# Two of eight gate pairs as plain products, a later spread of the roots, and tiles moved by 64 bytes

## The chip, the cores and the metric

The kernel runs on one core of one Trainium2 chip. The metric is the device time of one execution in microseconds (us); the time of a version is the median of its runs. TensorE (PE) does the matmuls, VectorE (DVE), ScalarE (ACT) and GpSimd (POOL) the rest, SyncE (SP) issues most DMAs. Each engine works through its own list of instructions in order, and waits on semaphores for the others.

## The reference

A trunk of two residual layers over 512 tokens of width 1024: a gMLP mixer, an MLP, a forgetting-attention mixer (FoX), an MLP, all float32. What is changed lies in the gMLP mixer (and, by its addresses, behind it):

```python
h = rms_norm(x, mix_norm_g[0])
z = gelu(h @ w_in)                    # (512, 4096)
u, v = split(z, 2, axis=-1)           # 2048 columns each
v = layer_norm(v, ln_g, ln_b)         # over the 2048 columns
s = einsum('gts,bnsgc->bntgc', tril(w_s), v) + b_s   # 128x128 over tokens, 8 groups
x = x + (u * s) @ w_out
```

Then `x = x + square(relu(rms_norm(x) @ w1)) @ w2`, the attention layer, and once more the MLP.

## The kernel before, in words

**Splitting.** Each float32 operand of a matmul is split into a high part (a copy by ACT, `wh`, `xh`, `th`, `zh`) and a low part (the difference, by DVE or POOL, `wl`, `xl`, `tl`, `zl`); a product is three matmuls, high by high, high by low, low by high (`mm3`, L275 for each matmul).

**The stream of weights.** `Stream` holds one list of weight chunks of 128 x 1024 (512 KB) for the whole kernel. `take()` hands out the next, keeps three more split ahead, and three loads ahead of those. Raw chunks have three places (`raw`), split ones four (`wh`, `wl`). L96 is a load, L99 the ACT half of a split, L100 the DVE half.

**Products by sevens.** Most products of the widening layers are made in pairs of 128 output rows by a scheme with seven products of half size (two blocks of rows, two halves of the depth, two halves of the 512 tokens) in place of eight. It needs sums of weight blocks and sums of token blocks. In the gMLP the weight sums are made on POOL in the places of the two raw chunks (`_sums_in_place`, L126 to L129), when the second chunk has been split ("end": only half of it is split for itself), and then count as two more chunks, "S31" and "S24". The token sums are `th`, `tl` (`gth`, `gtl` in the profile).

**The gMLP stage** goes in this order on TensorE: `pv`, the first half of the v columns in plain products, in two blocks `g` of four chunks `c`; within it the norm's sums of squares (`nps`, L317 to L329 with the root on POOL) and, four small multiplications, the spread of the roots over the partitions (`spread`, `npb`); `va` to `vd`, the second half of v by sevens; then what `GMLP_ORDER` lists. In that list `("uu", n, a, b, c, d)` is pair n of 128-column blocks of u by sevens (`gate_pair`, products `da` and `bc`, joined by DVE on L570 and L574, then scaled by the roots on L416 and put through gelu on L417), a to d being blocks whose mixing is issued behind the first two, the third and fourth, the fifth and sixth, and the seventh product. `("w", q)` loads mixing weights, `("s", n)` issues mixing n, and `("o", g, m)` is a chunk of the output product with blocks 4g to 4g+3 (`po`).

**A mixing** (`mix`) scales a block of v by the layer norm (`lnr`, `lnm`, ACT L623), splits it (`vh` ACT L626, `vl` POOL L627), multiplies by the mixing weights (`sp`, L640 and L641), applies gain and bias (`b` L630, `zt` L643 and L644 on DVE), multiplies by u (POOL L646) and splits the result (`zg` ACT L653, `zl` DVE L654). The load of `bs` on L618 serves two mixings.

**Order.** The program text is not the order on the engines: a planner sorts instructions by what its model of the engines holds ready, within the dependencies. The FoX stage is pinned.

**Places.** Tiles lie in pools, one behind another in each partition: `const`, `wp` (chunks), `xp` (x, `xh`, `xl`), `small`, and on top of these in turn `gp` with `vp` or `gq` (gMLP), `mp` (MLP) and `fs` with `fp` (FoX). A tile takes a multiple of 32 bytes in each partition, so the length of `small` sets the addresses in all pools behind it. In the program before, `small` ends at byte 123584, 192 past a multiple of 256; behind `lngb` (128 bytes), or a filling tile `pad`, the tiles follow at 64 past one.

```python
def take(self):
    i = self.taken
    self.prefetch(i + 1 + self.ahead)
    self.taken += 1
    return self.parts.pop(i)
```

Of the kernel before, what the change touches and what calls it, by code (L numbers as in the profile page):

```python
# [8 lines left out]
F32 = mybir.dt.float32  # L9
F32R = mybir.dt.float32r  # L10
AF = mybir.ActivationFunctionType
# [5 lines left out]
P = 128  # L17
# [3 lines left out]
NT = S // P  # L21
# [21 lines left out]
WARM = 8  # L43


GMLP_ORDER = [("w", 0), ("uu", 0, None, None, None, None), ("uu", 1, None, None, 0, None), ("uu", 2, None, 1, 2, None)]
GMLP_ORDER += [("uu", 3, 3, None, None, None), ("o", 0, 0), ("s", 4), ("o", 0, 1), ("s", 5), ("o", 0, 2), ("o", 0, 3)]
GMLP_ORDER += [("uu", 4, 6, 7, None, None), ("w", 1), ("o", 1, 0), ("o", 1, 1)]
GMLP_ORDER += [("uu", 5, 8, 9, None, None), ("o", 1, 2), ("o", 1, 3)]
# [118 lines left out]
def trunk(ctx: ExitStack, tc: tile.TileContext, A, out, stages=4):  # L168
# [10 lines left out]
    def psA(name):  # L179
        return ps.tile([P, S], F32, tag="A", name=name, bufs=4)  # L180
# [12 lines left out]
    chunks = []  # L193
# [5 lines left out]
    for q in (1, 2, 4, 3):  # L199
        chunks += [((q, c), None) for c in range(2)]  # L200
    for kind, *at in GMLP_ORDER:
        if kind == "uu":
            chunks += [(A["gw_u"][2 * at[0]], "begin"), (A["gw_u"][2 * at[0] + 1], "end"), ("S31", None), ("S24", None)]
        elif kind == "o":
            chunks += [A["gw_o"][at[0], at[1]]]
# [150 lines left out]
    def dense_a(dst, w, nm, pin=False):  # L356

        wh, wl = (t.rearrange("p (k m) -> p k m", m=P) for t in w)
        for k in range(KB):
            mm3(dst, wh[:, k], wl[:, k], nm.h[k], nm.l[k], k == 0, k == KB - 1, pin and k == 0)  # L360
# [26 lines left out]
    nm = Norm(0)  # L387
# [8 lines left out]
    with ExitStack() as st:  # L396
# [1 line left out]

        lngb = gp.tile([P, 2, E // P], F32, tag="lngb", name="lngb")
        nc.sync.dma_start(lngb, A["ln_gb"])  # L400
        onesr = gp.tile([P, P], F32R, tag="onesr", name="onesr")
        act.activation(onesr, ones, AF.Copy)

        v = [gp.tile([P, 4, NT, P], F32, tag=f"v{g}", name=f"v{g}") for g in range(4)]
        th, tl = ([gp.tile([P, 4, HS], F32R, tag=f"t{w}{k}", name=f"gt{w}{k}") for k in range(4)] for w in "hl")
        bn = small.tile([P, NT, 4, 6], F32, tag="bn", name="bn")
        tok = [slice(i * P, (i + 1) * P) for i in range(NT)]
        us = {}

        def u_place(b, dt, name):  # L410

            return gq.tile([P, S], dt, tag=f"u{b % 8}", name=f"{name}{b}")

        def gated(pu, u):

            dve.tensor_tensor(u, pu, nm.rbc, op=ALU.mult)  # L416
            act.activation(u, u, AF.Gelu_apprx_tanh)  # L417

        with ExitStack() as st2:
# [44 lines left out]
            for g in range(2):  # L464
                pv = [(psB if g == 1 and i < 3 else psA)(f"pv{g}_{i}") for i in range(NT)]
                for c in range(4):
                    wh, wl = (t.rearrange("p (k n) -> p k n", k=2) for t in ws.take())
                    for i in range(NT):
                        for kk in range(2):
                            k = 2 * c + kk  # L470
                            mm3(pv[i], nm.h[k][:, tok[i]], nm.l[k][:, tok[i]], wh[:, kk], wl[:, kk], k == 0, k == KB - 1)
                    if g == 0 and c == 2:
                        with tc.issue_after(fourth):
                            for b in range(KB):
                                nm.square(b)
                        nm.finish()
                    if g == 0 and c == 3:
                        nm.spread()
                        with tc.issue_after(nm.squared.ins):
                            for k in range(4):  # L480
                                token_sums(k)
                    if g == 0 and c > 1:
                        with tc.issue_after(ws.issued[2 * c + 2].ins):
                            load_parts(c - 2)
                    if g == 1 and c in (1, 2):
                        sum_parts(c - 1)
                for i in range(NT):
                    normal(i, g, blocks(pv[i]))
# [51 lines left out]
        dve.tensor_scalar(lnv, mv[:, :, 1], LN_EPS, None, op0=ALU.add)  # L540
        lnr = small.tile([P, NT], F32, tag="lnr", name="lnr")
        pool.tensor_tensor(lnr, lnv, mhalf[:, :NT], op=ALU.pow)
        lnm = small.tile([P, NT], F32, tag="lnm", name="lnm")
        lnm_made = dve.scalar_tensor_tensor(lnm, mv[:, :, 0], -1.0, lnr, op0=ALU.mult, op1=ALU.mult)

        def gate_pair(n):
# [52 lines left out]
        def mixing_weights(q):  # L599

            wT = small.tile([P, 4, P], F32, tag="sq", name=f"wsT{q}", bufs=2)
            nc.sync.dma_start(wT, A["w_sT"][4 * q : 4 * q + 4].rearrange("g s t -> s g t"))
            pool.affine_select(wT, wT, pattern=[[0, 4], [1, P]], compare_op=ALU.is_ge, fill=0.0, base=0, channel_multiplier=-1)
            wsb = gq.tile([P, 4, 2, P], F32R, tag="wsb", name=f"wsb{q}")
            pool.tensor_scalar(wsb[:, :, 0], wT, 1.0, None, op0=ALU.mult)
            pool.tensor_tensor(wsb[:, :, 1], wT, wsb[:, :, 0].bitcast(F32), op=ALU.subtract)
            now["w"] = wsb

        def mix(cb):
            g = cb // 2 % 4  # L610
            wsb = now["w"]
            if cb % 8 == 0:
                now["rs"] = psD(f"rs{cb}")
                for w in range(2):
                    pe.matmul(now["rs"].rearrange("p (g t) -> p g t", g=4), onesr, wsb[:, :, w], start=w == 0, stop=w == 1)
            if cb % 2 == 0:
                now["b"] = gq.tile([P, P], F32, tag="bs", name=f"bs{cb}", bufs=2)
                nc.sync.dma_start(now["b"], A["b_s"][cb // 2].partition_broadcast(P))  # L618

            vb = v[cb // 4][:, cb % 4]  # L620
            with tc.issue_after(now["vh"]) if cb else ExitStack():
                for i in range(NT):
                    act.activation(vb[:, i], vb[:, i], AF.Identity, scale=lnr[:, i : i + 1], bias=lnm[:, i : i + 1])  # L623
            vh = gq.tile([P, NT, P], F32R, tag="vh", name=f"vh{cb}", bufs=2)
            vl = gq.tile([P, NT, P], F32R, tag="vl", name=f"vl{cb}")
            now["vh"] = act.activation(vh, vb, AF.Copy).ins  # L626
            pool.tensor_tensor(vl, vb, vh.bitcast(F32), op=ALU.subtract)  # L627
            b2 = gq.tile([P, P], F32, tag="b2", name=f"b2{cb}", bufs=2)
            with tc.issue_after(lnm_made.ins):
                dve.scalar_tensor_tensor(b2, now["rs"][:, g * P : (g + 1) * P], lngb[:, 1, cb : cb + 1], now["b"], op0=ALU.mult, op1=ALU.add)  # L630
            zt = gq.tile([P, NT, P], F32, tag="zt", name=f"zt{cb}")
            wide = wsb[:, g].rearrange("p w t -> p (w t)")
            gcol = lngb[:, 0, cb : cb + 1]
            for c in range(2):

                sp = psA(f"sp{cb}_{c}")
                s4 = sp.rearrange("p (i w t) -> p i w t", i=2, w=2)
                for i in range(2):
                    dst = sp[:, i * 2 * P : (i + 1) * 2 * P]
                    pe.matmul(dst, vh[:, 2 * c + i], wide, start=True, stop=False)  # L640
                    pe.matmul(dst[:, :P], vl[:, 2 * c + i], wsb[:, g, 0], start=False, stop=True)  # L641
                zc = zt[:, 2 * c : 2 * c + 2]
                dve.scalar_tensor_tensor(zc, s4[:, :, 0], gcol, b2.unsqueeze(1).to_broadcast([P, 2, P]), op0=ALU.mult, op1=ALU.add)  # L643
                dve.scalar_tensor_tensor(zc, s4[:, :, 1], gcol, zc, op0=ALU.mult, op1=ALU.add)  # L644
            zf = zt.rearrange("p i t -> p (i t)")
            pool.tensor_tensor(zf, zf, us[cb], op=ALU.mult)  # L646

            if cb == 0:
                zg[0] = gq.tile([P, 4, S], F32R, tag="zg", name="zg0")
            elif cb % 4 == 0:  # L650
                zg[cb // 4] = gp.tile([P, 4, S], F32R, tag=f"v{cb // 4 - 1}", name=f"zg{cb // 4}")
            h, l = zg[cb // 4][:, cb % 4], u_place(cb, F32R, "zl")
            act.activation(h, zf, AF.Copy)  # L653
            dve.tensor_tensor(l, zf, h.bitcast(F32), op=ALU.subtract)  # L654
            z[cb] = (h, l)

        nxt = Norm(1)
        for kind, n, *at in GMLP_ORDER:
            if kind == "w":
                mixing_weights(n)  # L660
            elif kind == "uu":
                for _, cb in zip(gate_pair(n), at):
                    if cb is not None:
                        mix(cb)
            elif kind == "s":
                mix(n)
            else:
                zs = [z[4 * n + k] for k in range(4)]
                out_chunk(at[0], [t[0] for t in zs], [t[1] for t in zs], 4, 256, nxt.block if n == 3 else None)
# [142 lines left out]
    nm = fx  # L812
# [387 lines left out]
```

## Time and profile before

| | us |
|---|---|
| median of 3 runs | 1280.51 (1279.18 to 1280.64) |
| the profiled execution | 1282.32 |
| its span, first to last instruction | 1280.6 |
| TensorE busy | 1259.1 (98%) |
| VectorE busy | 903.5 (71%) |
| ScalarE busy | 686.0 (54%) |
| GpSimd busy | 524.0 (41%) |
| mean granted TensorE clock | 0.995 of full |

A row of the profile names line, engine, operation, output and inputs; a bracket at its end is the idle time of the engine before it and what ended that. The page gives the busy share of 40 equal slices as digits (9 is 90% or more), for the clock of TensorE the granted share. A line that is a helper's (L275, L99, L100) stands for many uses, which the tile names tell apart.

### The profile page before, as it was taken

What the parts mean: (1) busy time and instruction counts of PE and PEld (TensorE: products, weight loads), DVE (VectorE), ACT (ScalarE), POOL (GpSimd) and SP (SyncE); (2) the same over time, 40 slices, a digit from 0 to 9 for tenths busy, and PEclk for the clock granted to TensorE, in tenths of its full rate; (3) what the DMA queues carried; (4) which work ended last, traced back from release to release, by engine and by line L of the source; (5) the groups of instructions that cost most, each with busy time, mean ns of one, the idle gap of its engine ahead of it and who ended that gap; (6) DMA issues with size and microseconds to landing.
All of it is one profiled execution on the core that took longest, in us unless ns stands there. A gap on an engine that the chain in (4) does not pass through costs nothing.

```text
span 1280.6 us, 19160 instructions
## 1 busy us (share of the span) xinstructions
PE 1259.1 (98%) x7379; PEld 1122.6 (88%) x7379; DVE 903.5 (71%) x1196; ACT 686.0 (54%) x1125; POOL 524.0 (41%) x418
## 2 busy tenths in 40 slices
PE   9998899999999999999999999999999999999998
PEld 8788788988899989898899999898888999999987
DVE  7967877788876767666625666667897767676763
ACT  6666654645544443433457777778465444444430
POOL 3125546536333232310547666667273423223200
PEclk9998899999999999999999999999999999999999
DMA  8502332232332323242223223223213323232321
GB/s 284 190 19 83 104 93 70 90 129 78 116 116 83 118 81 127 72 131 83 70 88 120 86 87 97 86 83 115 91 66 116 112 87 115 83 115 83 116 83 66
DMA packets 42732, 129.08 MB, mean 101 GB/s; under 512 B 5320, under 2 KB 7424, under 8 KB 42640
## 3 DMA queue, kind: packets, MB, share of 16 engines
q1 hardware_dynamic: 42352, 127.83, 30.8%
q8 instruction: 58, 0.95, 0.3%
q14 instruction: 34, 0.28, 0.1%
q10 hardware_dynamic: 288, 0.02, 0.0%
HBM read 125.67 MB, written 2.16 MB: 100 GB/s over the span
## 4 chain that ended last, share of the span: by engine, by line
PE 82%; DVE 7%; POOL 3%; issue 3%; ACT 2%; DMA 1%; SPq 0%; DVEq 0%; POOLq 0%; ACTq 0%
PE po L275 35%; PE da L275 13%; PE bc L275 10%; PE pq L275 9%; PE pg L275 3%; PE ph L275 3%; DVE wl L100 2%; PE pv L275 2%; PE ot L275 2%; PE lg L275 1%; PE va L275 1%; PE tp L280 1%; PE vc L275 1%; ACT wh L99 1%; POOL zt L646 1%
## 5 line engine op out<-in xcount | busy, mean ns | idle before, releaser
L99 ACT ACTIVATE wh<-raw 128x1024 fp32r<-128x1024 f32 (+3 forms) x244 | 229.8, 947 | 199.0 <-PE po L275 82.1
L100 DVE TENSOR_TENSOR wl<-raw,wh 128x1024 fp32r<-128x1024 f32 (+1 forms) x192 | 274.1, 1442 | 24.1 <-ACT wh L99 23.5
L275 PE MATMUL po<-zl,wh 128*128 128x512 f32 x640 | 251.8, 394 | 1.4 <-DVE zl L710 1.4
L275 PE MATMUL po<-zh,wl 128*128 128x512 f32 x512 | 201.9, 394 | 0.0
L275 PE MATMUL po<-zh,wh 128*128 128x512 f32 x512 | 199.6, 391 | 0.0
L766 DVE TENSOR_TENSOR x<-x,po 128x512 f32<-128x512 f32 x128 | 87.3, 683 | 105.9 <-PE po L275 105.9
L100 POOL TENSOR_TENSOR wl<-raw,wh 128x768 fp32r<-128x768 f32 (+3 forms) x52 | 103.2, 1986 | 125.0 <-ACT wh L99 122.5
L139 POOL TENSOR_TENSOR ssum<-raw 128x512 f32<-128x512 f32 x26 | 34.9, 1344 | 273.1 <-DMA raw<-in_m_dram 251.7
L99 ACT ACTIVATE sh<-ssum 128x1024 fp32r<-128x1024 f32 x52 | 55.2, 1061 | 163.1 <-issue 93.2
L275 PEld LDWEIGHTS po<-zl,wh 128*128 128x128 f32 x640 | 120.8, 189 | 24.0 <-DVE zl L710 1.6
L275 PEld LDWEIGHTS po<-zh,wl 128*128 128x128 f32 x512 | 96.4, 188 | 19.0
L275 PEld LDWEIGHTS po<-zh,wh 128*128 128x128 f32 x512 | 96.4, 188 | 18.2
L275 PE MATMUL pq<-wh,xh 128*128 128x384 f32 (+2 forms) x256 | 88.2, 344 | 0.0
L275 PE MATMUL pq<-wh,xl 128*128 128x384 f32 (+2 forms) x256 | 83.1, 325 | 0.0
L275 PE MATMUL pq<-wl,xh 128*128 128x384 f32 (+2 forms) x256 | 82.9, 324 | 0.0
L100 DVE TENSOR_TENSOR sl<-ssum,sh 128x1024 fp32r<-128x1024 f32 x52 | 66.0, 1268 | 18.1 <-ACT sh L99 18.0
L141 POOL TENSOR_TENSOR ssum<-raw,ssum 128x512 f32<-128x512 f32 x26 | 37.2, 1429 | 65.1 <-DVE sl L100 64.8
L275 PE MATMUL da<-th,sl 128*128 128x256 f32 x208 | 59.0, 283 | 0.0
L275 PE MATMUL da<-th,sh 128*128 128x256 f32 x208 | 58.8, 282 | 0.0
L275 PE MATMUL da<-tl,sh 128*128 128x256 f32 x208 | 58.7, 282 | 0.0
L746 DVE TENSOR_TENSOR zc<-da,sl 128x512 f32<-128x512 f32 x26 | 18.0, 692 | 55.1 <-PE da L275 55.1
L142 POOL TENSOR_TENSOR ssum<-raw,raw 128x512 f32<-128x512 f32 x26 | 56.3, 2164 | 0.0
(288 smaller groups left out, 3660.3 us busy)
## 6 DMA issues: line engine op xcount, KB each, us to landing
raw<-in_m_dram SPq DMA_DIRECT2D x128, 512.0 KB, 3.8
raw<-in_gw_u_dram SPq DMA_DIRECT2D x16, 512.0 KB, 3.5
raw<-in_gw_o_dram SPq DMA_DIRECT2D x16, 512.0 KB, 3.6
raw<-in_fw_qkv_dram SPq DMA_DIRECT2D x20, 384.0 KB, 3.1
raw<-in_gw_v_dram SPq DMA_DIRECT2D x12, 512.0 KB, 5.7
gs<-in_gw_v_dram SPq DMA_DIRECT2D x8, 512.0 KB, 7.9
raw<-in_fw_g_dram SPq DMA_DIRECT2D x8, 512.0 KB, 3.6
cb<-cd SPq DMA_DIRECT2D x16, 256.0 KB, 3.4
```

The costliest lines, as they stand in the source:

```text
L99: self.nc.scalar.activation(hi, t, AF.Copy)
L100: eng.tensor_tensor(lo, t, hi.bitcast(F32), op=ALU.subtract)
L139: tt(s12[:, 0], a21, a22, op=ALU.add)
L141: tt(s43[:, 0], a12, s12[:, 1], op=ALU.subtract)
L142: tt(s43[:, 1], a11, a21, op=ALU.subtract)
L275: ins = pe.matmul(dst, a, b, start=start, stop=stop, skip_group_check=more)
L280: placed(pe.transpose(dst, src, ident[: src.shape[0], : src.shape[0]]), 256)
L646: pool.tensor_tensor(zf, zf, us[cb], op=ALU.mult)
L746: dve.tensor_tensor(z[:, 1].rearrange("p (j t) -> p j t", j=2), a.unsqueeze(1).to_broadcast([P, 2, HS]), late.rearrange("p (j t) -> p j t" ...
L766: dve.tensor_tensor(x[b], x[b], pt, op=ALU.add)
```

## The change

- Pairs 0 and 2 of the gate blocks become plain: `("u", n, a, b)` takes one chunk for each block of 128 columns, makes the product with all 512 tokens into one bank (`pu`, `dense_a`, 24 matmuls of 512 columns), and scales and gelus it from there. Their chunks are listed for plain splitting, without sums.
- Mixing 0 is issued behind the fourth part of pair 1, 1 and 2 behind the two products of pair 2. Before, 0 stood behind the third part of pair 1, 1 and 2 behind the second and third of pair 2.
- `spread` is issued in block g = 1 behind chunk c = 1, before in block g = 0 behind chunk c = 3.
- `onesr` is placed behind `v`, `th` and `tl`, and `lnm` is written into the tile of `lnv`, so that `small` is 64 bytes shorter.

```diff
-GMLP_ORDER = [("w", 0), ("uu", 0, None, None, None, None), ("uu", 1, None, None, 0, None), ("uu", 2, None, 1, 2, None)]
+GMLP_ORDER = [("w", 0), ("u", 0, None, None), ("uu", 1, None, None, None, 0), ("u", 2, 1, 2)]
...
     for kind, *at in GMLP_ORDER:
-        if kind == "uu":
+        if kind == "u":
+            chunks += [A["gw_u"][2 * at[0] + e] for e in range(2)]
+        elif kind == "uu":
...
-        onesr = gp.tile([P, P], F32R, tag="onesr", name="onesr")
-        act.activation(onesr, ones, AF.Copy)
-
         v = [gp.tile([P, 4, NT, P], F32, tag=f"v{g}", name=f"v{g}") for g in range(4)]
         th, tl = ([gp.tile([P, 4, HS], F32R, tag=f"t{w}{k}", name=f"gt{w}{k}") for k in range(4)] for w in "hl")
+        onesr = gp.tile([P, P], F32R, tag="onesr", name="onesr")
+        act.activation(onesr, ones, AF.Copy)
...
+                    if g == 1 and c == 1:
+                        nm.spread()
                     if g == 0 and c == 3:
-                        nm.spread()
...
-        lnm = small.tile([P, NT], F32, tag="lnm", name="lnm")
+        lnm = lnv
...
+            elif kind == "u":
+                for b, cb in enumerate(at, 2 * n):
+                    pu = psA(f"pu{b}")
+                    dense_a(pu, ws.take(), nm)
+                    us[b] = u_place(b, F32, "u")
+                    gated(pu, us[b])
+                    if cb is not None:
+                        mix(cb)
```

More of the change, by code (lines that the diff above doesn't have):

```diff
@@ L400, in trunk @@
         nc.sync.dma_start(lngb, A["ln_gb"])
+        v = [gp.tile([P, 4, NT, P], F32, tag=f"v{g}", name=f"v{g}") for g in range(4)]
+        th, tl = ([gp.tile([P, 4, HS], F32R, tag=f"t{w}{k}", name=f"gt{w}{k}") for k in range(4)] for w in "hl")
         onesr = gp.tile([P, P], F32R, tag="onesr", name="onesr")
         act.activation(onesr, ones, AF.Copy)
-        v = [gp.tile([P, 4, NT, P], F32, tag=f"v{g}", name=f"v{g}") for g in range(4)]
-        th, tl = ([gp.tile([P, 4, HS], F32R, tag=f"t{w}{k}", name=f"gt{w}{k}") for k in range(4)] for w in "hl")
         bn = small.tile([P, NT, 4, 6], F32, tag="bn", name="bn")
```

## The prediction

> **What bounds the kernel now.** I read the page first, then the waits of TensorE, then a table of stretches around the place that they point to, then the chain of waits and the timelines there. The page says that TensorE is busy nearly all the time:
>
> ```profile
> span 1280.6 us, 19160 instructions
> PE 1259.1 (98%) x7379; PEld 1122.6 (88%) x7379; DVE 903.5 (71%) x1196; ACT 686.0 (54%) x1125; POOL 524.0 (41%) x418
> PEclk9998899999999999999999999999999999999999
> ```
>
> So there are three ways to a shorter time: fewer or shorter matmuls, less of the 21.5 us in which TensorE is idle (1280.6 less 1259.1), and the two slices (the fourth and fifth, 96 to 160 us) in which the granted clock is under full. The waits of TensorE between 100 and 152 us, in total, times and longest:
>
> ```profile
> PE da L275 <- DVE wl L100: 3.3, 2, 2.8
> PE da L275 <- ACT wh L99: 2.3, 2, 1.9
> PE sp L640 <- DVE zt L644: 2.1, 1, 2.1
> PE bc L275 <- DVE wl L100: 0.5, 1, 0.5
> ```
>
> `wh` and `wl` are the two parts into which a weight chunk is split, `da` and `bc` the products of a gate pair, `sp` a mixing. The stretches (us, then busy us and instructions of PE, PEld, DVE, ACT, POOL, then the granted clock):
>
> ```profile
> 91.60:104.40 12.80, 12.80 (x107) 12.70 (x106) 12.73 (x22) 7.08 (x13) 5.25 (x6) 1.00 0.27 83
> 104.40:112.90 8.50, 5.71 (x40) 4.75 (x39) 5.88 (x11) 8.50 (x18) 5.83 (x4) 1.00 0.21 69
> 112.90:119.80 6.90, 5.51 (x26) 5.51 (x27) 5.11 (x5) 4.74 (x12) 5.06 (x4) 0.51 0.24 76
> 119.80:140.20 20.40, 17.45 (x142) 16.77 (x142) 18.05 (x23) 12.92 (x25) 13.17 (x10) 1.00 0.20 56
> 140.20:143.70 3.50, 3.50 (x19) 3.50 (x19) 1.66 (x3) 3.03 (x8) 3.50 (x2) 0.51 0.27 23
> 143.70:147.10 3.40, 1.54 (x12) 1.34 (x12) 3.06 (x7) 1.96 (x3) 2.63 (x3) 1.00 0.32 133
> 147.10:150.50 3.40, 3.40 (x15) 3.11 (x14) 3.40 (x3) 2.77 (x6) 1.69 (x2) 0.50 0.44 72
> 150.50:260.00 109.50, 108.64 (x681) 97.62 (x681) 84.99 (x124) 59.18 (x106) 55.74 (x39) 1.00 0.32 100
> ```
>
> From 104.4 to 150.5 us TensorE idles 2.79 + 1.39 + 2.95 + 1.86 = 9.0 us, and 5.51 + 3.50 + 3.40 = 12.4 us of its work run at half clock, which loses half of that, 6.2 us. Before and after it hardly waits. These 15.2 us are the gate pairs 0 to 3 and the mixings 0 to 3, and the change rewrites just that.
>
> **The change part by part: pairs 0 and 2 as plain products.** A plain pair is 2 x 8 x 3 = 48 matmuls of 512 columns; a pair by seven products is 7 x 4 x 3 = 84 of 256. Pieces of the chain of waits (start, us, what) price both:
>
> ```profile
> 53.02 5.44 PE va L275 x24
> 69.50 5.60 PE vc L275 x24
> ...
> 149.11 2.14 PE po L275 x6
> ...
> 323.04 5.48 PE ph L275 x24
> ...
> 1234.28 1.44 PE da L275 x12
> 1235.72 1.39 PE bc L275 x12
> ...
> 1241.30 35.74 PE po L275 x156
> ```
>
> `ph` is the plain product of the MLP with the same operands (weights against `xh`, `xl`): 48 matmuls are 10.96 us. 84 at 1.44/12 = 0.120 are 10.08. Two pairs: **+1.8 us** of TensorE work, on the path since TensorE is the bound.
>
> What goes with it is off TensorE: for each of the two pairs four sums on POOL, two splits of 1024 columns on ACT and DVE, two joins on DVE and four copies on ACT, against half a split more, as the second chunk is now split whole. What a split costs DVE alone, what beside POOL, and what that does to TensorE:
>
> ```profile
> 76.72 1.23 DVE L100 TENSOR_TENSOR wl<-gs,wh 128x1024 fp32r<-128x1024 f32 x1 [2.00 <-ACT wh L99]
> 111.99 5.07 DVE L100 TENSOR_TENSOR wl<-raw,wh 128x1024 fp32r<-128x1024 f32 x3
> 114.29 0.58 PE L275 MATMUL da<-gth,wl 128*128 128x256 f32 x1 [2.85 <-DVE wl L100]
> 128.36 0.39 PE L275 MATMUL da<-gth,wl 128*128 128x256 f32 x1 [0.42 <-DVE wl L100]
> 139.69 0.39 PE L640 MATMUL sp<-wsb,vh 128*128 128x256 f32 x1 [2.15 <-DVE zt L644]
> 143.77 1.72 POOL L129 TENSOR_TENSOR raw<-raw 128x512 f32<-128x512 f32 x1
> 146.63 0.38 PE L275 MATMUL da<-gth,wh 128*128 128x256 f32 x1 [1.86 <-ACT wh L99]
> ```
>
> The wait of 2.85 is for pair 1's last chunk of sums, which stood on DVE behind the mixing; the 0.42 is pair 2's; the 1.86 is pair 3's, whose fourth sum ended on POOL only at 145.5. Now pair 0 needs no sums. Pair 1's can be made as soon as its two chunks are there, under 10.96 us of plain product, and a chunk feeds 5.5 us of TensorE, not 1.4 to 2.9: the waits for `wh` and `wl` up to 128.4 go (2.79 + 1.39 + 0.42 = 4.6), and with them the first half-clock stretch (2.75): **-7.35 us**. Bounds: 0, if they come back under the new order, and all of it.
>
> Behind that, pair 3 stays as it is, but pair 2 in front of it asks nothing of POOL. With 11 us of plain product ahead, its sums can be ready some microseconds early (its two chunks land while pair 2 begins, the four sums are 4 x 1.7, the splits need slots that pair 2's own chunks leave at its middle and end). I let the 1.86 and one half-clock stretch (half of 3.50) go: **-3.6 us**. The `sp` wait of 2.15, its companions (0.4) and the other half-clock stretch I leave: it comes from DVE, which had 18.05 us of work in 20.4. The bounds of this part are 0 and 7.8.
>
> The clock: it was halved at 112.9 behind a wait of 2.85, at 140.2 behind 2.15, at 147.1 behind 1.86. The Trainium skill, page "TensorE: Matmul & The Clock Gate", section "HAM oscillation — how this bites in real kernels", has a rule against gaps of over about 3.4 us. The trace differs: no gap here is that long, and the clock fell thrice. By that rule the half-clock stretches would not hang on these waits, and the two terms would be 4.6 and 1.86, a gain 4.5 us smaller.
>
> **The mixings.** Mixing 0 moves from behind the third product of pair 1 to behind the fourth, 1 and 2 behind the two plain products of pair 2. All their instructions (on ACT four scalings and two copies, on DVE six operations, on POOL two, on TensorE eight matmuls and two more for the first, on SP one small load for each two) stay the same in number: 0. They are hidden by the 11 us of pair 2; without that cover each is a wait like the 2.15 above. On SP the small load must not fall behind a chunk load that waits for a slot; there that costs up to
>
> ```profile
> 108.39 16.49 SPq L96 DMA_DIRECT2D raw<-in_gw_u_dram  x3
> ```
>
> three loads over 16.5 us. What waits for it is DVE's `b` in a mixing, and all splits queued behind that.
>
> **The roots spread later.** Now TensorE stands before the third piece of the roots:
>
> ```profile
> 36.87 1.16 PE L275 MATMUL npb<-ident,rstd 128*128 128x128 f32 x8 [0.94 <-POOL rstd L329]
> ```
>
> Moved behind two more chunks of 24 matmuls (10.9 us), the four multiplications find `rstd` ready: **-0.9 us**. Their own 0.9 us and the copy on ACT stay. What could take its place is the next matmul's own wait, for the split of chunk 4 or for a bank; the split is done long before, and three of the four banks of the second block are others than the first's, so I take the full 0.94. Bounds: 0 and 1.1.
>
> **The addresses.** With `lnm` written over `lnv`, the pool `small` loses two 32-byte places. By the address table of the program before, the tiles of `gp`, `gq`, `vp`, `mp` and `fp` start 64 bytes past a multiple of 256, those of `wp` and `xp` on one; now all start on one. `onesr`, 512 bytes, moves the rest by whole multiples: nothing. Does an address cost anything? In the chain above `va` (from `xh`, on the boundary) is 5.44 and `vc` (from `th`, off it) 5.60, with weights alike: 6.7 ns a matmul, for 96 of them 0.6 us. `po`, whose moving operand `zh` or `zl` is off, has 229.1 ns; on it stand `ph` with 228.3 and `va` with 226.7. The counts:
>
> ```profile
> L275 PE MATMUL po<-zl,wh 128*128 128x512 f32 x640 | 251.8, 394 | 1.4 <-DVE zl L710 1.4
> L275 PE MATMUL po<-zh,wl 128*128 128x512 f32 x512 | 201.9, 394 | 0.0
> L275 PE MATMUL po<-zh,wh 128*128 128x512 f32 x512 | 199.6, 391 | 0.0
> ...
> L275 PE MATMUL bc<-xh,sh 128*128 128x256 f32 x104 | 29.1, 280 | 0.0
> ```
>
> 1664 x 0.8 to 2.4 ns is 1.3 to 4.0 us; I take the middle, 2.7, as neither row is the nearer. Against it: the fast 256-column group (1.39 for 12, `xh` with `sh`) has one operand on and one off, the slow one (1.44) both alike; 3 x 104 matmuls that go from the one to the other lose 4.2 ns each, 1.3 us. Together **-2.0 us**; bounds +1.3 and -4.6.
>
> The Trainium skill, page "SBUF — State Buffer", sections "Operand start alignment" and "Who interferes with whom", asks only for element alignment and gives TensorE two read ports that wait for no one. By it this part is 0; the trace's 5.60 beside 5.44 speaks against that.
>
> **The sum.** +1.8 - 7.35 - 3.6 - 0.9 - 2.0 = -12.05 us. The profiled execution took 1282.32 us, span 1280.6 and 1.7 around it: 1270.3. The median of the runs is 1.8 below that execution: **1268.4 us**.
>
> **The rivals.**
> - The later half stays. Pair 3 keeps its sums and DVE its load (18 of 20 us), the 3.6 us don't come: 1272.0. For it: the `sp` wait isn't of the removed work. Against: POOL loses half of its sums there.
> - All goes. The whole 15.2 us are regained and the addresses give the upper bound: 1268.4 less 4.2 less 2.6, 1261.6. For it: beyond 150.5 us, with pairs of the same kind but more matmuls beside them, only 0.9 us in 109.5 are idle.
> - The clock is halved there whatever the waits are, and stays so: the half-clock parts of the two terms (2.75 and 1.75) don't come, 1272.9. Against: the clock is full over the 109.5 us behind, with 0.9 us idle. The Trainium skill's rule above would say this.
> - Addresses don't matter: 1270.4. For it: unlike operands in the rows above; against: 5.60 beside 5.44.
> - Slower: SP stands before a chunk load that waits for a slot, with the small load of mixing 0 behind it; DVE waits in its queue, all splits with it. As long as the 16.49 us above, wholly on TensorE, it gives 1268.4 + 16.5 = 1284.9. It decides from 12.1 + 2.6 = 14.7 us on. Against: chunks now keep their place for one split, not for sums.
> - The waits only move to the first output product, which needs mixings 0 to 3: all of the 11 us come back there, and the time is 1279.4, no change.
>
> **How the numbers follow.** The forecast (waits mostly gone, 1264 to 1271) has 0.50, the later half staying 0.17, all going 0.12, the clock staying low 0.03, the addresses being nothing 0.06, no change 0.05, slower 0.07. 1268.4 is the likeliest. A measurement here tells some 0.2%, 2.6 us, from no change. Faster: 0.50 + 0.17 + 0.12 + 0.03 + 0.06 = 0.88; same 0.05; slower 0.07. The range goes from just under the case in which all goes, 1261, to 1276, where half of the 7.35 also stays: it leaves out the last two cases and little else.
>
> **What would show it.** In the profile after, between 90 and 140 us: no wait of TensorE on `wl` over 1 us and the clock digit of the fourth and fifth slice at 9; the first `po` in the chain some 10 us earlier than 149.1; eight POOL sums of raw up to pair 3 in place of sixteen; no wait for `rstd`; `vc` and `va` from `th` at 5.44 for 24; the `po` run of 156 at the end under 35.74. Wrong I am if TensorE waits for `sp`, `zl` or `wh` by turns in each pair and the clock stays halved, or if the 5.60 stay 5.60.

## The result, and the profile after

| | before | after |
|---|---|---|
| median of 4 runs, us | 1280.05 (1279.18 to 1280.64) | 1271.64 (1271.41 to 1271.99) |
| profiled execution | 1282.32 | 1271.42 |
| its span | 1280.6 | 1269.5 |
| mean granted clock | 0.995 | 0.999 |

The ratio of the times is 0.9935, with an interval of 0.9918 to 0.9952: faster by some 0.65%. A second comparison of the same two kernels, on another chip, gave 1271.02 beside 1280.84, 0.9918 (0.9905 to 0.9932). Each ratio, here and below, is the estimate on record with its interval; it can differ by some 0.1% from the quotient of the two medians. The forecast of 1268.4 was 3.2 us too low; the range held the time.

The page of after, its span, its engines and its clock digits:

```profile
span 1269.5 us, 18988 instructions
PE 1253.6 (99%) x7307; PEld 1117.6 (88%) x7307; DVE 889.3 (70%) x1188; ACT 680.8 (54%) x1113; POOL 509.4 (40%) x410
PEclk9999999999999999999999999999999999999999
```

The two low digits of before are gone, and TensorE is idle for 15.9 us (1269.5 less 1253.6) in place of 21.5. What it waits for between 100 and 152 us (engine, tile and line, what ended the wait, total, times, longest):

```profile
PE po L277 <- DVE x L375: 2.1, 1, 2.1
PE da L277 <- ACT gsl L559: 1.1, 1, 1.1
PE sp L644 <- POOL vl L630: 0.4, 1, 0.4
```

Before, the four groups shown in the prediction summed to 8.2 us, all but 2.1 of it for `wh` and `wl` (two more, of 0.3 each, stood behind them). No wait for a split of weights is left; `vl` is the low half of a block of v in a mixing. The stretches of the same stage (us, busy us and instructions of PE, PEld, DVE, ACT, POOL, granted clock, DMA share, GB/s):

```profile
89.70:109.20 19.50, 18.37 (x108) 16.20 (x106) 14.09 (x26) 13.55 (x27) 9.35 (x7) 1.00 0.18 58
109.20:148.00 38.80, 38.41 (x243) 34.77 (x244) 29.78 (x42) 26.83 (x50) 18.48 (x13) 1.00 0.31 93
148.00:151.30 3.30, 1.15 (x7) 0.85 (x6) 3.30 (x8) 2.56 (x6) 2.67 (x2) 1.00 0.73 245
151.30:154.70 3.40, 3.40 (x10) 2.63 (x9) 1.98 (x3) 0.65 (x2) 0.00 (x0) 0.50 0.05 20
154.70:260.00 105.30, 104.84 (x656) 94.38 (x654) 82.22 (x120) 54.98 (x96) 55.76 (x38) 1.00 0.33 100
```

What is left there is 1.13 us of waiting at 109.2, 0.39 in the second row, 2.15 in the third, and one stretch of 3.40 us at half clock, which loses 1.7: 5.4 us in place of 15.2. DVE's timeline shows what the wait of 2.15 is for:

```profile
143.25 0.68 DVE L577 TENSOR_TENSOR u<-da,gsl 128x512 f32<-128x512 f32 x1
143.85 2.33 DVE L100 TENSOR_TENSOR wl<-raw,wh 128x1024 fp32r<-128x1024 f32 x1
146.11 0.86 DVE L646 SCALAR_TENSOR_TENSOR zt<-sp,lngb,b 128x256 f32<-128x256 f32 x2
146.89 1.21 DVE L100 TENSOR_TENSOR wl<-raw,wh 128x1024 fp32r<-128x1024 f32 x1
148.03 0.68 DVE L418 TENSOR_TENSOR u<-u,rbc 128x512 f32<-128x512 f32 x1
148.63 0.86 DVE L647 SCALAR_TENSOR_TENSOR zt<-sp,lngb,zt 128x256 f32<-128x256 f32 x2
149.41 0.33 DVE L633 SCALAR_TENSOR_TENSOR b<-rs,lngb,bs 128x128 f32<-128x128 f32 x1
149.67 1.86 DVE L375 TENSOR_TENSOR x<-x,po 128x512 f32<-128x512 f32 x3
```

No row has a bracket: DVE works without a gap through pair 3's last join, its scaling, two splits of weights and operations of a mixing, and only then adds the finished output products to `x` and so empties the bank that the next `po` needs.

Where the time went is told by stage. Each column is the distance between two starts of matmuls in the profiled execution, in us: from the first of the norm's sums (`nps`) to the first `va`; v by sevens, from the first `va` to the last; the gate stage, from the last `va` to the first `ph`; the first MLP, from the first `ph` to the first `pg`; and the whole span. The runs of the next section stand in the same table.

| kernel | nps to va | v by sevens | gate stage | first MLP | span |
|---|---|---|---|---|---|
| before | 24.84 | 38.52 | 196.91 | 346.16 | 1280.6 |
| after | 24.84 | 37.85 | 187.39 | 346.13 | 1269.5 |
| after, second profile | 24.33 | 37.85 | 185.68 | 346.13 | 1266.9 |
| before + plain pairs | 24.98 | 38.52 | 187.59 | 346.16 | 1270.7 |
| before + addresses | 24.98 | 37.85 | 196.39 | 346.13 | 1279.0 |
| before + later spread | 24.72 | 38.52 | 197.20 | 346.16 | 1280.0 |
| before + pair 0 plain | 24.60 | 38.52 | 189.93 | 346.16 | 1273.7 |
| after + sums off by 64 | 24.42 | 37.85 | 185.74 | 344.93 | 1265.3 |
| after + sums off by 128 | 24.23 | 37.85 | 186.18 | 346.25 | 1268.0 |
| after + mean first | 23.67 | 37.85 | 185.63 | 346.13 | 1266.6 |
| after + pair 3 plain | 24.78 | 37.85 | 184.02 | 346.13 | 1265.8 |
| after + all three | 23.64 | 37.85 | 183.59 | 344.93 | 1262.0 |

### The profile page after: what moved, and what is told of

Read it like the earlier page. It is cut to its first block, busy times and chain, and to the rows that moved or that the text cites. A ratio compares the mean times of both kernels' runs of the same rounds, so it can differ in the third digit from the quotient of the medians.

```text
span 1269.5 us, 18988 instructions
## 1 busy us (share of the span) xinstructions
PE 1253.6 (99%) x7307; PEld 1117.6 (88%) x7307; DVE 889.3 (70%) x1188; ACT 680.8 (54%) x1113; POOL 509.4 (40%) x410
## 4 chain that ended last, share of the span: by engine, by line
PE 80%; DVE 5%; ACT 2%; POOL 2%; issue 2%; DMA 0%; POOLq 0%; DVEq 0%
PE po L277 35%; PE da L277 13%; PE bc L277 10%; PE pq L277 9%; PE pg L277 3%; PE ph L277 3%; PE ot L277 2%; PE lg L277 2%; DVE xl L305 1%; PE tp L282 1%; DVE wl L100 1%; PE pv L277 1%; ACT wh L99 1%; POOL zt L649 0%; PE sp L643 0%
## 5 line engine op out<-in xcount | busy, mean ns | idle before, releaser
L99 ACT ACTIVATE wh<-raw 128x1024 fp32r<-128x1024 f32 (+3 forms) x240 | 226.6, 949 | 203.8 <-PE po L277 85.5
L100 DVE TENSOR_TENSOR wl<-raw,wh 128x1024 fp32r<-128x1024 f32 (+1 forms) x188 | 265.3, 1424 | 28.9 <-ACT wh L99 28.6
```

The lines of the kernel that those rows point to most:

```text
L99: self.nc.scalar.activation(hi, t, AF.Copy)
L100: eng.tensor_tensor(lo, t, hi.bitcast(F32), op=ALU.subtract)
```

## The experiments

The first four runs take the change apart: each adds one part of it to the kernel before. They ran on one chip, where before had 1281.36.

**The plain pairs alone**, with the mixings' new places (the branch for `"u"` is that of the change):

```diff
-GMLP_ORDER = [("w", 0), ("uu", 0, None, None, None, None), ("uu", 1, None, None, 0, None), ("uu", 2, None, 1, 2, None)]
+GMLP_ORDER = [("w", 0), ("u", 0, None, None), ("uu", 1, None, None, None, 0), ("u", 2, 1, 2)]
```

> The kernel before with only the plain pairs 0 and 2 and their order of mixings. If the gate stage carries nearly all of the gain (theory A): 7.5 to 9.5 us faster than before, the first block of the MLP 9 to 10 us after the last va closer, the v stage (va to its end, 38.5 us) unchanged. If the addresses carry some 2 us of it, as predicted (theory B): only 6 to 7 us faster. If the spread carries 0.9 (theory C): 0.9 less than the whole change.

1271.11 us, 0.9931 (0.9919 to 0.9944): this part alone gives what the change gives. Its gate stage lasts 187.59 us, after's 187.39. Its largest waits of TensorE from 26 to 160 us are after's two, and still the old one for the roots:

```profile
PE po L277 <- DVE x L375: 2.2, 1, 2.2
PE da L277 <- ACT gsl L558: 1.1, 1, 1.1
PE npb L277 <- POOL rstd L331: 1.1, 1, 1.1
```

**Pair 0 alone as plain**, pairs 1 and 2 and all mixings as before (one entry of `GMLP_ORDER`, with the same branch):

```diff
-("uu", 0, None, None, None, None),
+("u", 0, None, None),
```

> The kernel before with pair 0 alone plain, mixings as before. By my walk the waits up to 119.8 us and the first half-clock stretch go (6.9), for 0.9 of more matmuls: -6 us, and the rest of the gain, 2 to 3 us, belongs to pair 2. If the later half depends on pair 2 and the first on both: -2 to -4 us, with a half-clock stretch still there behind pair 1.

1275.16 us, 0.9959 (0.9945 to 0.9972). The gate stage falls by 7.0 us, to 189.93; pair 2, with the mixings' places, gives the other 2.3 (187.59). The four largest waits from 100 to 160 us of this kernel:

```profile
PE da L277 <- ACT wh L99: 2.0, 1, 2.0
PE sp L642 <- DVE zt L646: 1.3, 1, 1.3
PE da L277 <- ACT gsl L558: 1.0, 1, 1.0
PE da L277 <- DVE wl L100: 0.7, 1, 0.7
```

With pair 2 still by sums, a wait for `wh` just before pair 3's last products (2.0 us, of the size of the 1.86 of before) and one for `zt` ahead of it (1.3) stay; with pair 2 plain both are gone. So the second plain pair, together with the mixings' new places, does remove the later waits, as the step said; no run has the one without the other.

**The addresses alone:**

```diff
-        onesr = gp.tile([P, P], F32R, tag="onesr", name="onesr")
-        act.activation(onesr, ones, AF.Copy)
         v = [...]
         th, tl = (...)
+        onesr = gp.tile([P, P], F32R, tag="onesr", name="onesr")
+        act.activation(onesr, ones, AF.Copy)
...
-        lnm = small.tile([P, NT], F32, tag="lnm", name="lnm")
+        lnm = lnv
```

> The kernel before with only the addresses moved by 64 bytes. Theory A: v stage 0.65 us shorter (38.5 to 37.85), each MLP within 0.2 us of before, because po gains about 1.3 ns a matmul and the 256-column products lose about as much in all; total -0.5 to -1.0. Theory B: -2.0 in all, -0.7 or more in each MLP. Addresses mean nothing: 0, and the groups of 24 stay 5.60.

1279.81 us, 0.9993 (0.9985 to 1.0002): no difference that can be told. The stages show why it isn't simply nothing. The chain of this run has the products from `th` at the pace of those from `xh`:

```profile
58.08 5.44 PE vb L275 x24
...
68.96 5.44 PE vc L275 x24
```

`vc` had 5.60, and v by sevens is 0.67 us shorter. But the MLP stays at 346.13 us.

**The later spread alone:**

```diff
+                    if g == 1 and c == 1:
+                        nm.spread()
                     if g == 0 and c == 3:
-                        nm.spread()
```

> The kernel before with only the spread of the roots moved. Theory A: 0 (within 0.3 us), the wait of 0.9 us for rstd replaced by one of about 0.9 for a bank of the second block, which the gelu of the first block frees, and that needs rstd too. Theory C: -0.9 us and no wait between 34 and 42 us.

1281.16 us, 1.0001 (0.9992 to 1.0010): nothing. TensorE's timeline of this kernel has `npb` without a wait, and at the time at which `npb` waited before (36.87) a wait at a product of the next block:

```profile
36.79 0.50 PE L275 MATMUL pv<-wh,xh 128*128 128x512 f32 x1 [0.78 <-ACT v L461]
40.10 1.05 PE L275 MATMUL npb<-ident,rstd 128*128 128x128 f32 x8
```

The second group of runs starts from the kernel after and goes at what the first group left: the MLP that did not move, the wait that took the place of the roots', and the wait for `x`. Three of them and after itself once more ran on another chip (before: 1280.84); the kernel with sums off by 128 bytes and the one with all three parts ran on a third (before: 1281.08).

> The changed kernel again, on the same chip as the three that start from it: 8 to 9 us faster than before.

1271.02 us (1268.73 to 1271.29), 0.9918 (0.9905 to 0.9932). Its profile has the same waits in the gate stage, 2.1 for `x` among them, and yet no half-clock stretch behind:

```profile
148.00:151.30 3.30, 1.15 (x8) 0.92 (x7) 3.30 (x8) 2.47 (x7) 2.66 (x2) 1.00 0.83 243
151.30:154.70 3.40, 3.40 (x17) 2.77 (x16) 3.20 (x6) 1.47 (x3) 0.00 (x0) 1.00 0.11 45
```

The same 3.30 us with 1.15 of work were followed by clock 0.50 in one execution and by 1.00 in the other. That is the 1.7 us by which the two gate stages differ. The five executions of this run fall apart accordingly: 1268.73 and 1269.18 us with a mean clock of 1.000, 1271.02 to 1271.29 with 0.998 or 0.999. A median thus also depends on how many of its executions had the stretch, so the runs below are compared by their stages first.

**The sums' splits off the boundary.** A filling tile puts the split weight sums of the MLP (`sh`, `sl`) 64 bytes past a multiple of 256, and in a second kernel 128:

```diff
+        if self.sums_pad:
+            nc.vector.memset(sp.tile([P, self.sums_pad], F32, tag="off", name=f"off{i}", bufs=1), 0.0)
+            self.sums_pad = 0
...
-            ws.sums_pool = mp
+            ws.sums_pool, ws.sums_pad = mp, 16   # 16 words, 64 bytes; 32 words in the second kernel
```

> The changed kernel with the split sums of weights of the MLP (sh, sl) alone put 64 bytes off a multiple of 256, all else on one. If a moving operand on the boundary with a next stationary operand 64 off it is the fast pair (theory A, from the groups of 12 at 1.39 against 1.44): about 1200 matmuls of 256 columns go from 119.7 to some 116 ns, each MLP 2 us shorter, 4 us in all below the changed kernel. If addresses do nothing and the unchanged MLP time was no balance of two effects (theory B): 0 within 0.5 us.

> The changed kernel with the split sums of the MLP 128 bytes off a multiple of 256 instead of 64. If what matters is that next stationary and moving operand differ in their place within 256 bytes: each MLP 1.2 us or more below the changed kernel, as at 64. If 64 is special, or only multiples of 128 count as on the boundary: MLP time as in the changed kernel, 346.1.

With 64 bytes 1267.81 us, 0.9894 (0.9881 to 0.9908); the first MLP is 1.20 us shorter, and the second 1.25 (348.19 in after, 346.94 here, with the same wait of 1.3 us for `zl` in both; in the second profile of after, where that wait was 0.2, it lasted 347.13). That is less than the 2 us that were expected for each MLP. With 128 bytes 1269.97 us, 0.9918 (0.9905 to 0.9932), the ratio of after itself, and the first MLP is not shorter (346.25): the expectation that any difference in place within 256 bytes would do is refuted. The chain in the first MLP, twelve products with the sums at a time, of after, of 64 bytes and of 128 bytes:

```profile
517.85 1.43 PE da L277 x12
519.28 1.44 PE bc L277 x12
```

```profile
515.32 1.42 PE da L280 x12
516.74 1.41 PE bc L280 x12
```

```profile
516.45 1.45 PE da L280 x12
517.90 1.44 PE bc L280 x12
```

**The mean first.** On DVE the mean of squares `ms` goes ahead of the token sums and sums of chunks that stood before it:

```diff
-            dve.tensor_scalar(self.ms, ...)
+            self.mean = dve.tensor_scalar(self.ms, ...)
...
-                        with tc.issue_after(nm.squared.ins):
+                        with tc.issue_after(nm.squared.ins), tc.issue_after(nm.mean.ins):
...
-                        sum_parts(c - 1)
+                        with tc.issue_after(nm.mean.ins):
+                            sum_parts(c - 1)
```

> The changed kernel with the sums of tokens and of weight parts queued on DVE behind the mean of squares (ms), so that the root is made earlier. If the wait of 0.9 us at 36.7 is for the root through the bank (theory A): ms 3 to 4 us earlier, no wait between 26 and 45 us, 0.9 us below the changed kernel. If the bank is held by something else: the wait stays, 0.

1268.42 us, 0.9899 (0.9885 to 0.9912). DVE's timeline, after and then this kernel:

```profile
32.65 0.16 DVE L329 TENSOR_SCALAR ms<-nps 128x4 f32<-128x4 f32 x1
```

```profile
28.17 0.16 DVE L329 TENSOR_SCALAR ms<-nps 128x4 f32<-128x4 f32 x1 [1.42 <-PE nps L277]
```

`ms` stands 4.5 us earlier, now behind `nps` itself; the waits of TensorE list none between 20 and 100 us, and the stretch from `nps` to `va` is 23.67 us in place of 24.84 or 24.33.

**Pair 3 plain too:**

```diff
-("uu", 3, 3, None, None, None)
+("u", 3, 3, None)
```

> The changed kernel with pair 3 plain too, mixing 3 behind its first product. More matmuls: +0.9 us. If the wait of 2.15 us at 150 and the half clock behind it (1.7) come from DVE's work for pair 3 (theory A): -3 us net. If DVE is as full without it: +0.9, slower than the changed kernel.

1267.70 us, 0.9895 (0.9882 to 0.9909). Two waits are left between 20 and 170 us:

```profile
PE da L277 <- ACT gsl L559: 1.1, 1, 1.1
PE pv L277 <- ACT v L463: 0.9, 1, 0.9
```

The wait for `x` is gone, and with it the half-clock stretch: the four executions lie within 1 us of each other. The gate stage is 184.02 us, 1.7 below the one of after that had no such stretch and 3.4 below the one that had it, though the pair costs more TensorE work.

**All three** of these in one kernel:

> The changed kernel with all three: split sums of the MLP 64 bytes off, the mean of squares ahead on DVE, pair 3 plain. If the three act in places of their own, their stage gains add: MLP 2.4 us, roots 1.2, gate stage 1.7, together 5 us below the changed kernel, about 1265 to 1266. If the early root or the plain pair shifts the others' order: 2 to 3 us only.

1264.01 us (1263.73 to 1265.42), 0.9871 (0.9857 to 0.9884): 17 us below before (1281.08 there), and the best version here. Each stage is as short as in the run of its own part: 23.64, 183.59 and 344.93 us. The expected 5 us are what separates it from the two executions of after without the half-clock stretch (4.7 and 5.2); from after's median it is 7.0. TensorE's waits from 4 to 300 us are few:

```profile
PE da L280 <- ACT gsl L563: 1.1, 1, 1.1
PE da L280 <- DVE wl L100: 0.4, 1, 0.4
PE pv L280 <- ACT wh L99: 0.3, 1, 0.3
```

## Why the prediction was right, and where it was off

**Direction and place: right.** The gain is all in the gate stage, and the plain pairs alone make it. The terms for it were +1.8 - 7.35 - 3.6 = -9.15 us; the stage is 9.5 us shorter in the profiled executions, 9.3 with the plain pairs alone. The rows account for it less closely than that agreement suggests: idle time and half clock fall by 9.8 us (15.2 to 5.4) up to 154.7, waiting behind it by 0.4, and +1.8 of matmuls should leave 8.4. Put the other way, idle time and half clock fell by 10.2 us and the stage by 9.5, so TensorE's work there grew by some 0.7 us where the sum had +1.8; why the two pairs cost so much less, no run shows. So the close agreement of 9.15 and 9.5 is in part luck.

**The first term (7.35).** The waits for `wh` and `wl` up to 128.4 and the first half-clock stretch are gone, as it said; 1.13 us came back as a wait for ACT's copy of a product out of its bank (`gsl`), which the step did not name. Pair 0 alone, with 0.9 us more of matmuls by the forecast, gave 7.0, where 7.35 less 0.9 is 6.45. But that is not this term alone: behind 130 us that kernel has one half-clock stretch (138.75 to 142.16 us) where before had two, so some 1.9 us of its gain belong to the next term's part. Which engine's relief counts, POOL's sums, DVE's splits and joins or ACT's copies, no run separates. The step also read the clock as falling behind the wait of 2.85; it fell at 112.94, in the middle of that wait (111.44 to 114.29), and the last section says what decides.

**The second term (3.6).** The 1.86 is gone and so is the stretch behind it. What the step left standing, a wait of 2.15 from DVE with a half-clock stretch, is there in size and in cause, but at another place: the `sp` wait shrank to 0.39, and DVE, busy without a gap, now holds up the first bank of `po` instead. With pair 3 plain the wait is gone, so it hangs on pair 3's being made by sevens; that it does so through DVE is what DVE's timeline suggests, and no run separates it.

**The spread (-0.9): wrong.** The multiplications for the spread no longer wait, as said, but the step dismissed what would come next: "three of the four banks of the second block are others than the first's". TensorE's timeline of after has the matmul on the fourth bank ahead of all:

```profile
36.74 0.50 PE L277 MATMUL pv<-wh,xh 128*128 128x512 f32 x1 [0.90 <-ACT v L463]
40.06 1.05 PE L277 MATMUL npb<-ident,rstd 128*128 128x128 f32 x8
```

That bank is emptied by the first block's gelu, which needs the same roots. Moving the consumer left the late producer where it was: `ms` at 32.65. Moving that gave 1.2 us (24.84 to 23.67), or 0.7 against the second profile.

**The addresses (-2.0): mis-sized.** The term was -0.6 in v, -2.7 in `po`, +1.3 in products of 256 columns. v by sevens gave 0.67. In the MLPs the two others cancel: 346.16 to 346.13 us with the move alone. The chain's run of 156 near the end shows that the gain in `po` is there, smaller than taken:

```profile
1230.52 35.40 PE po L277 x156
```

It was 35.74; over all 776 `po` matmuls of the first MLP the mean distance of two starts falls from 229.7 to 228.6 ns, 0.9 us, so some 1.8 in both MLPs. The products of 256 columns lost as much: over the 1092 `da` and `bc` matmuls of the first MLP the mean distance rises from 118.7 to 119.6 ns, 1.0 us, some 2.0 in both MLPs. The step had 1.3 for the kernel, from three groups of 104; the rows of 12 above show `bc` with the sums at 1.44 where before had 1.39. With the sums set apart from the tokens by 64 bytes the mean is 118.5 ns and the MLP 1.2 us shorter. So the rival "addresses don't matter" has the time of the MLPs right and the mechanism wrong. The Trainium skill's page "SBUF — State Buffer", section "Operand start alignment", asks only for element alignment, and says that this is about legality and not about speed; that this term would be 0 by it was too much to read from it. What a shift of 64 bytes costs these runs show: 0.67 us in v by sevens and 1.2 in an MLP.

**The sum.** With the terms as measured (-9.5, 0, -0.7) the change is -10.2 us where -12.05 was forecast; the profiled executions differ by 10.9. Another 1.0 us lies ahead of the stages: the first `nps` starts at 28.02 us in before and at 27.02 in after, but at 27.73 in the second profile of after, so this is the start of an execution and not the change. The rest of the miss lies in the starting point: the profiled execution of before stood 1.8 us above the median known then (1280.51), which the forecast took off again, and that of after stood 0.2 below its own. The two executions of after that came within 0.8 us of the forecast, 1268.73 and 1269.18, did so by luck: they lack a half-clock stretch that the forecast had left standing. The medians of the two comparisons differ by 8.4 and 9.8.

**The rivals.** "The later half stays" gave 1272.0, nearer to 1271.64 than the forecast, but not its mechanism: the gate stage alone would have fallen by 5.55 us, and fell by 9.5. "The clock stays low" and "no change" are refuted by the clock digits and the gate stage. The slower case would have shown as a wait of several microseconds for a split or a mixing; the longest left is the 2.15 for `x`. "All goes" was held off in the gate stage above all by the wait for `x`, which pair 3 plain removes.

## What to carry to other kernels

A trick that saves TensorE work can cost more than it saves where the engines that prepare its operands are full: here 1.8 us more of matmuls by the forecast, some 0.7 by the trace, bought 10 us less of waiting and half clock. Before moving a late result's consumer, look for the next consumer of the same result, and move the producer if you can. Compare a change by stage, not by the whole time: two parts here cancelled to nothing in one stage, and a rival came nearer to the total than the forecast while its mechanism was absent.

## What the runs showed of the hardware

The clock behind one and the same wait of 2.15 us fell to half in one execution (0.50 from 151.3 to 154.7 us) and not in another (1.00), which is worth 1.7 us; the executions of after on that chip lie in two groups, 2 us apart. The Trainium skill, page "TensorE: Matmul & The Clock Gate", section "What's actually happening", has the gate watch a free-running window of about 3.4 us; the traces agree. Within each of the twelve traces all changes of the clock lie whole steps of 3.413 us apart, up to its fall behind the last work: in after at 151.27, 154.68 and 1270.84. So the steps can be counted back to the wait. In after one step holds all of it (148.25 to 150.40); in the second profile of after, whose clock falls only at 1265.93, an edge at 149.77 cuts it (148.43 to 150.58). The stretches of the two, in the columns of above:

```profile
147.86:151.27 3.41, 1.26 (x8) 0.96 (x8) 3.41 (x8) 2.58 (x7) 2.67 (x2) 1.00 0.73 244
```

```profile
146.36:149.77 3.41, 2.07 (x13) 1.70 (x11) 3.41 (x8) 2.07 (x4) 1.17 (x1) 1.00 0.59 174
149.77:153.18 3.41, 2.60 (x11) 2.16 (x12) 3.41 (x6) 2.37 (x6) 1.50 (x2) 1.00 0.43 136
```

Over the twelve traces, behind their start, every such step at full clock in which TensorE worked 1.57 us or less was followed by half clock, and none in which it worked 1.63 us or more. So here it was not the length of one wait that counted, but the idle time that fell into one step.

The place of an operand within 256 bytes changes the pace of these products by two or three per cent: 24 of 512 columns take 5.44 us with both operands on a multiple of 256 and 5.60 with the token sums 64 bytes past one; 12 of 256 columns take 1.44 us with both on it and 1.41 with the weight sums 64 bytes past one. So the layout that is fast for the one is the slow one for the other, and 128 bytes did not act like 64. Why is open; the runs show only which layouts are fast.
